# Transposes of both halves of a piece in one visit, with new planner rules and a reordered opening

## The chip, the cores and the metric

The kernel runs on one core of one Trainium2 chip. The metric is the device time of one execution in microseconds (us), the median of several runs. TensorE (PE in the profile, PEld for its weight loads) multiplies matrices and writes PSUM, VectorE (DVE), ScalarE (ACT) and GpSimd (POOL) work element by element, and SyncE (SP) issues most DMAs.

## The reference

One block of a hybrid sequence model over 1040 tokens (16 learned ones and 1024 frames) of width 1024: a mixer with four mLSTM heads and four retention heads, and a gated MLP with a causal convolution of three taps. Cut to what matters here:

```python
h = concat([meta, x])                                   # (1, 1040, 1024)
h = h + token_mixer(rmsnorm(h, norm_mix_g), ...)
h = h + channel_mixer(rmsnorm(h, norm_ffn_g), ...)
return rmsnorm(h, norm_final_g)[:, 16:]

def token_mixer(u, ...):
    proj = u @ w_in              # per head: q, k (128 wide), v (256), o or g (256), mLSTM gates
    ...
    h_ml = sigmoid(ml_o) * head_norm(mlstm_chunkwise(q, k, v, li, lf), ml_norm_g)
    h_rt = silu(rt_g) * head_norm(retention_chunkwise(rq, rk, rv, log_gamma), rt_norm_g)
    return concat([h_ml, h_rt]) @ w_out

def channel_mixer(u, ...):
    return (silu(causal_dwconv(u @ w_up, ffn_conv_w)) * (u @ w_gate)) @ w_down
```

The recurrences carry a 128 x 256 state per head from chunk to chunk; `head_norm` takes mean and variance over the 256 values of a head.

## The kernel before, in words

**Products.** Tokens lie along the free dimension, features along the 128 partitions. Each float32 operand is split into a high part (`hi`, a ScalarE copy to float32r) and a low part (`lo`, a VectorE subtraction), and each product is made of three float32r matmuls, hi x hi, lo x hi and hi x lo (`mm3`, `mm3s`, L889 to L903). The large products go through a scheme of seven block products in place of eight (`wino_fm`, `v_steps`, later `Seven` and `seven`), with the weights' sums made on VectorE (`quartered`, L553). The scan of the heads, the transposes and the norms' sums use plain float32 matmuls.

**The opening (L1735 to L1810).** Five column ranges (`RNG`, L251: 144 and 128 columns first) are normalised one after the other. `norm_sums(r)` (L848) squares the inputs on ScalarE and VectorE, adds the squares, sums over partitions by matmuls (`pca`, L824), and takes a square root and a reciprocal (L826, L827). `norm_split(r)` (L872) spreads the result over the partitions by matmuls (`pra`, L836), scales the columns (L879) and splits them (L880, L884). `v0_split` (L905) splits head 4's value weights; the low parts `w0lo` are subtracted on GpSimd. `v4_group(c)` (L919) makes the values of chunk c from them: high columns times high weights, high times low, then low times high; in group 1 the call `between`, which is `norm_sums(1)`, stands ahead of the last third. `need(("q4", 0), 1)` calls for the query weights' parts (`parts`, L472; the subtractions are the `lo_q` of L479). `last[...]` keeps an instruction, and `after(x, last[...])` orders x behind it on its engine without a semaphore. In this part the framework's own scheduler fixes the order on each engine, by readiness and place in the program.

**The planner (L1815 to L1917).** From head 4's output gate on, the kernel's own planner deals out the work. A model (`watch`, L132) follows the engines' loads with a price per instruction; on TensorE each change between float32 and float32r matmuls is charged (L178). Between products (`slot`, L1701) tasks from the list `side` are started, first come first served, if the task's own condition holds. A rule from `RULES` is in force for each stage (output gate `o`, query and key `q`, value `v`, `vp`, by head or pair). Its seven numbers are: how many weight parts ahead count as near, how long ahead of its data a waiting task may be resumed, the backlog of VectorE and ScalarE from which other pending tasks wait, the backlog from which no new task is started, the most tasks per slot, the order of the queues, and the most tasks with matmuls per slot. `done` holds what the model thinks finished, and when. `drain(nm, keep)` forces all but the last `keep` tasks.

**The scan.** For head h and each of nine chunks, `scan_a` (L1508) makes scores and `scan_b` (L1551) the state update `u` (bank "upd") and the output `n` (bank "num"). PSUM has eight banks: two each for `pa` and `pb` (products), one each for `sA`, `num`, `upd` and `tr`. After the chunks of one of three pieces (`PIECES`: 400, 384 and 256 tokens), `post_steps` (L1591) takes the head norm's statistics (`stats`) and then, per half b of the 256 features, `half(b)` (L1623): the chunks' outputs are transposed on TensorE into the bank `tr`, VectorE multiplies them with the norm's weight and the gate (`mix_into`, L1637) into a buffer `mx` (three of them), and ScalarE's queue stores it to DRAM (`mxd`, L1655). Head 7's mixes go straight to the operands of the next product (`wact`). Each half starts when bank `tr` is free by the model and its half of the gate (`sig`) is ready.

Of the kernel before, what the change touches and what calls it, by code (L numbers as in the profile page):

```python
# [47 lines left out]

RULE = (3, 0.5, 3.0, 2.5, 2, 0, 1)
RULES = {  # L50
# [19 lines left out]
}  # L70

# [18 lines left out]
def body(ctx, tc, h_in, vecs, cst, mask_in, rot, w_v0, w_vp, w_g, w_out, w_up, w_gate, w_down, out):  # L90
# [41 lines left out]
    def watch(ins):  # L132
# [25 lines left out]
        if dma:  # L158
            load[eng] = t + (0.4 if eng == "SP" else 0.1)
            size = n * o.ap[0][1] * 4e-6  # L160
            if eng == "SP":
                load["wire"] = max(load["wire"], t + 1.8) + size / 0.3 * (2 if "scr" in str(rd) else 1)
                end = load["wire"]
            else:
                load["wire"] += size / 0.3
                end = t + 1.8 + size / 0.15
        else:
            if eng == "PE":
                if F32 not in [x.dtype for x in ins.ins]:
                    c = max(0.107, 0.004 + 0.000445 * n)  # L170
                elif o.ap[0][1] == 32:
                    c = 0.13
                elif getattr(ins, "is_transpose", False):
                    c = 0.109
                else:
                    c = 2 * max(0.11, 0.00084 * n)
                whole = F32 in [x.dtype for x in ins.ins]
                c += 0.1 * (whole != kindof[0])  # L178
                kindof[0] = whole
                end = t + c + 0.165  # L180
            elif eng == "DVE":
                c = 0.07 + 0.00105 * n + (0.06 if "ScalarPtr" in kind else 0.0)
                end = t + c + 0.085
            elif eng == "Activation":
                c = 0.045 + 0.00093 * n + 0.1 * (len(ins.ins) - 1)
                f = ins.func.name if hasattr(ins, "func") else "Copy"
                if f in TABLES and f != table[0]:
                    table[0] = f
                    c += 1.3
                end = t + c + 0.1  # L190
            else:
                c = 0.15 + 0.0017 * n
                end = t + c
            load[eng] = t + c
            fin[0] = max(fin[0], end)
# [276 lines left out]
    def parts(key, pairs, src):  # L472
        for i, (hi, lo) in enumerate(pairs):
            m = AC.copy(hi, src[:, i * HB:(i + 1) * HB])
            if not dealt[0]:
                after(m, last["first"])
        yield
        for i, (hi, lo) in enumerate(pairs):
            V.tensor_tensor(lo, src[:, i * HB:(i + 1) * HB], hi.bitcast(F32), ALU.subtract)  # L479
        done.add(key)  # L480

    def pairs_of(nm, n):
# [365 lines left out]
    def norm_sums(r):  # L848
        half, j0, j1 = RNG[r]
        n = j1 - j0  # L850
        xs = [xf[f"{half + 1}{i + 1}"][:, :, j0:j1] for i in (0, 1)]
        sq = [x[:, :, j0:j1] for x in sqs]
        m = AC.activation(sq[0], xs[0], AF.Square)
        if r:
            after(m, last["sqrt"])
        if r < 2:
            m = V.tensor_tensor(sq[1], xs[1], xs[1], ALU.mult)
            if r:
                after(m, last["scale"])
        else:  # L860
            after(AC.activation(sq[1], xs[1], AF.Square), last["sqrt"])
        if r == 1:
            ss = [x[:, k] for x in sq for k in range(4)]
        else:
            m = V.tensor_tensor(sq[0], sq[0], sq[1], ALU.add)
            if r:
                after(m, last["recip"])
            V.tensor_tensor(sq[0][:, 0:2], sq[0][:, 0:2], sq[0][:, 2:4], ALU.add)
            ss = [sq[0][:, k] for k in range(2)]
        norms[r] = xs, rms_sums(ss[0], 0, n, f"a{r}", tmp.tile([P, 5], F32, tag="rcol", name=f"rcola{r}"), "tr", ss[1:])  # L870

    def norm_split(r):  # L872
# [4 lines left out]
        for i, x in enumerate(xs):  # L877
            for k in range(4):
                last["scale"] = V.scalar_tensor_tensor(x[:, k], x[:, k], vec[:, V_MIX + 4 * i + k:V_MIX + 4 * i + k + 1], pr, ALU.mult, ALU.mult)  # L879
            m = AC.copy(parts_[i][0], x)  # L880
            if r == 0:
                last["first"] = m
        for x, (h_, l_) in zip(xs, parts_):
            last["pace"] = V.tensor_tensor(l_, x, h_.bitcast(F32), ALU.subtract)  # L884
        if r == 0:
            for i, x in enumerate(xs):
                V.tensor_copy(ug[:, 4 * i:4 * i + 4], x[:, :, :32])
# [17 lines left out]
    def v0_split():  # L905
        for i in range(2):
            after(AC.copy(w0hi[i], w0raw[i]), last["sqrt"])
            G.tensor_tensor(w0lo[i], w0raw[i], w0hi[i].bitcast(F32), ALU.subtract)

    def quads(dst, pv, n):  # L910
        yield
# [639 lines left out]
    def scan_b(h, c):  # L1551
# [12 lines left out]
        num, mv, den = outs[p]  # L1564
        num.append(v_chunk(h, c, nv))
        if c < NCH - 1:
            up = pp(f"u{h}_{c}", "upd")
            PE.matmul(up[:, :nv], kw[:L], v, start=True, stop=True)  # L1568
        pn = pp(f"n{h}_{c}", "num")
# [4 lines left out]
        if c < NCH - 1:  # L1574
# [3 lines left out]
            else:  # L1578
                r = c * H + h
                d = dec[:, r:r + 1] if h < H else float(np.exp(lg[h - H] * P))  # L1580
                V.scalar_tensor_tensor(C[:, :nv], state["C"][:, :nv], d, up[:, :nv], ALU.mult, ALU.add)
            state["C"] = C
        AC.copy(num[slot][:L], pn[:L, :nv])
        if h < H:
            G.tensor_copy(den[:L, c:c + 1], num[slot][:L, DV:VW])
# [5 lines left out]
    def post_steps(h, p):  # L1591
# [28 lines left out]
            m["num"] = num  # L1620
            done.add(("z", h, p))

        def half(b):  # L1623
            num = m["num"]
            done.discard("tr")
            tr = ps.tile([P, 512], F32, tag="tr", name=f"tr{h}_{p}_{b}")
            for i, c in enumerate(chs):
                c0, L = CH[c]
                PE.transpose(tr[:, c0 - t0:c0 - t0 + L], num[i][:L, b * P:(b + 1) * P], ident[:L, :L])  # L1629
            yield  # L1630
            a0 = max(t0, KEEP)
            w = t1 - a0
            g = (V_MLG if h < H else V_RTG) + (h % H) * 2 + b
            i = 2 * h + b

            def mix_into(dst, x0, x1):
                return V.scalar_tensor_tensor(dst, tr[:, x0 - t0:x1 - t0], vec[:, g:g + 1], sig(b, p)[:, x0 - a0:x1 - a0], ALU.mult, ALU.mult)  # L1637
            if h == 7:
                for q, o in (("A2", MA), ("B2", MB)):
                    x0, x1 = max(a0, o), min(t1, o + HB)  # L1640
                    if x0 < x1:
                        mix_into(wact(q, 6 + b)[:, x0 - o:x1 - o], x0, x1)
                if t1 > MB + HB:
                    scanned["mix", b] = mix_into(mm[:, i], MB + HB, t1)
                done.add("tr")
                return
            mx = mxp.tile([P, WMAX], F32, tag="mx", name=f"mx{h}_{p}_{b}", bufs=3)
            mix_into(mx[:, :w], a0, t1)
            done.add("tr")
            e = min(t1, MB + HB)  # L1650
            if e < t1:
                V.tensor_copy(mm[:, i], mx[:, e - a0:w])
                posted.add(i)
            yield from settle()
            AC.dma_start(mxd[i][:, a0 - MA:e - MA], mx[:, :e - a0])  # L1655
            stored.add((i, p))
        return [(stats, 0, lambda: ("n", h, chs[-1]) in done)] + [(lambda b=b: half(b), 1, lambda b=b: done.can(("z", h, p), "tr") and ("sig", h, b) in done and "meta" not in done) for b in range(2)]

    side = []

    def tasks(h):
# [4 lines left out]

        def rb(c):
            v = [("v", h, int(c > 4))] if h not in (4, 7) else []
            return lambda: (h, c) in pre and done.can(("pre", h, c), *(turn if c == 0 else [("n", h, c - 1)] + v))
        A = [(lambda c=c: scan_a(h, c), 1, ra(c)) for c in range(NCH)]  # L1670
        B = [(lambda c=c: scan_b(h, c), 1, rb(c)) for c in range(NCH)]
        posts = [post_steps(h, p) for p in range(3)]
# [76 lines left out]
    norm_sums(0)  # L1749
    v0_split()  # L1750
    norm_split(0)
    v4_group(1, next(ring0), lambda: norm_sums(1))
    need(("q4", 0), 1)
    norm_split(1)
    v4_group(0, next(ring0))
    v4_group(2, next(ring0))
    norm_sums(2)
# [65 lines left out]
        return [(f, 0, lambda: "gates" in done)]  # L1823
    reset()
    load.update({"DVE": 7.0, "Activation": 5.5})
    done["tr"] = 0.0
    pinned[0] = True
    before.clear()
    go(o_steps(4))
    for p, (a, b) in enumerate(PAIRS):  # L1830
# [25 lines left out]
        go(steps[10:12])  # L1856
        side += cv[1:2]
        go(steps[12:])
        drain(f"sig{a}", 4)
        scan, halves_ = tasks(b)  # L1860
        if b < H:
            side += cv[2:3] + scan[:3] + cv[3:] + scan[3:10]
# [668 lines left out]
```

## Time and profile before

| | us |
|---|---|
| median of 3 runs | 1527.99 (1526.26 to 1529.33) |
| the profiled execution | 1527.2 |
| its span, first to last instruction | 1525.4 |
| TensorE busy | 1489.9 (98%) |
| VectorE busy | 1090.1 (71%) |
| ScalarE busy | 755.6 (50%) |

The profiled execution took 1.8 us more than its span, and 0.8 less than the median. The granted TensorE clock is 0.994 over the span. The rows of the views say which engine an instruction ran on, its line in the kernel, what it writes and reads, its start and its length; what stands in brackets at a row's end is how long its engine had been idle, and what ended that. Starts of matmuls are exact; their lengths overlap, since they are pipelined, so a matmul's price is read from start to start. A transpose on TensorE is a matmul, too.

### The profile page before, as it was taken

What the parts mean: (1) busy time and instruction counts of PE and PEld (TensorE: products, weight loads), DVE (VectorE), ACT (ScalarE), POOL (GpSimd) and SP (SyncE); (2) the same over time, 40 slices, a digit from 0 to 9 for tenths busy, and PEclk for the clock granted to TensorE, in tenths of its full rate; (3) what the DMA queues carried; (4) which work ended last, traced back from release to release, by engine and by line L of the source; (5) the groups of instructions that cost most, each with busy time, mean ns of one, the idle gap of its engine ahead of it and who ended that gap; (6) DMA issues with size and microseconds to landing.
All of it is one profiled execution on the core that took longest, in us unless ns stands there. A gap on an engine that the chain in (4) does not pass through costs nothing.

```text
span 1525.4 us, 25488 instructions
## 1 busy us (share of the span) xinstructions
PE 1489.9 (98%) x9929; PEld 1350.0 (88%) x9929; DVE 1090.1 (71%) x2087; ACT 755.6 (50%) x1453; POOL 73.6 (5%) x153
## 2 busy tenths in 40 slices
PE   6999999999999999999999999999999999999997
PEld 6998999999999999986888988999999999888887
DVE  7785868678777677856867787767666666778657
ACT  4465655554655455553454565444444444444443
POOL 1000000000000000000000001222220000000000
PEclk9999999999999999999999999999999999999999
DMA  6022255323532355696333247888772224933313
GB/s 232 8 88 51 86 159 194 111 82 114 186 119 98 125 166 189 195 398 255 111 112 134 80 124 241 197 208 200 189 183 77 83 79 160 369 105 110 97 42 111
DMA packets 104586, 223.81 MB, mean 147 GB/s; under 512 B 10520, under 2 KB 33760, under 8 KB 104288
## 3 DMA queue, kind: packets, MB, share of 16 engines
q1 hardware_dynamic: 89824, 191.68, 37.7%
q0 software_dynamic: 8448, 23.07, 7.6%
q10 hardware_dynamic: 6192, 7.41, 1.4%
q8 instruction: 78, 1.28, 0.4%
q14 instruction: 44, 0.36, 0.1%
HBM read 178.05 MB, written 67.15 MB: 161 GB/s over the span
## 4 chain that ended last, share of the span: by engine, by line
PE 89%; DVE 6%; DMA 2%; ACT 2%; issue 1%; SPq 0%; DVEq 0%; ACTq 0%
PE pdx L902 3%; PE pdx L901 3%; PE pdx L900 3%; PE pup_x L901 2%; PE pup_x L902 2%; PE pga_x L900 2%; PE pup_x L900 2%; PE pga_x L901 2%; PE pga_x L902 2%; PE pdy L902 2%; PE pdy L901 2%; PE pdy L900 2%; PE n L1570 2%; PE pwx L902 2%; PE u L1568 2%; PE pv L940 2%
## 5 line engine op out<-in xcount | busy, mean ns | idle before, releaser
L780 ACT CAST hi_up<-raw_up 128x512 fp32r<-128x512 f32 (+1 forms) x52 | 36.4, 719 | 107.4 <-PE pga_z L901 61.1
L781 DVE TENSOR_TENSOR lo_ga<-fraw_ga,hi_ga 128x512 fp32r<-128x512 f32 (+1 forms) x52 | 41.9, 809 | 37.3 <-ACT hi_ga L780 37.1
L781 DVE TENSOR_TENSOR lo_up<-raw_up,hi_up 128x512 fp32r<-128x512 f32 (+1 forms) x52 | 41.3, 810 | 38.0 <-ACT hi_up L780 37.2
L900 PE MATMUL pup_x<-uh_g,hi_up 128*128 128x256 f32 (+1 forms) x240 | 67.2, 282 | 1.2 <-ACT uh_g L1928 1.2
L901 PE MATMUL pup_x<-ul_g,hi_up 128*128 128x256 f32 (+1 forms) x240 | 67.4, 282 | 0.1
L902 PE MATMUL pup_x<-uh_g,lo_up 128*128 128x256 f32 (+1 forms) x240 | 66.4, 282 | 0.0
L781 DVE TENSOR_TENSOR lo_d<-rd,hi_d 128x1024 fp32r<-128x1024 f32 (+1 forms) x34 | 37.7, 1114 | 32.8 <-ACT hi_d L780 32.7
L780 ACT CAST hi_ga<-fraw_ga 128x512 fp32r<-128x512 f32 (+1 forms) x52 | 36.4, 719 | 45.3 <-PE pup_z L901 21.9
L902 PE MATMUL pdx<-uh_d,lo_d 128*128 128x512 f32 (+1 forms) x156 | 57.9, 375 | 0.0
L901 PE MATMUL pdx<-ul_d,hi_d 128*128 128x512 f32 (+1 forms) x156 | 57.8, 374 | 0.0
L780 ACT CAST hi_d<-rd 128x1024 fp32r<-128x1024 f32 (+1 forms) x34 | 32.3, 959 | 49.3 <-PE pdy L901 32.5
L902 PE MATMUL pdy<-uh_d,lo_d 128*128 128x512 f32 x132 | 51.9, 393 | 0.0
L901 PE MATMUL pdy<-ul_d,hi_d 128*128 128x512 f32 x132 | 51.7, 392 | 0.0
L900 PE MATMUL pdx<-uh_d,hi_d 128*128 128x512 f32 (+1 forms) x156 | 48.5, 372 | 0.0
L900 PE MATMUL pdy<-uh_d,hi_d 128*128 128x512 f32 x132 | 47.9, 389 | 0.0
L900 PE MATMUL pga_x<-uh_g,hi_ga 128*128 128x512 f32 x120 | 47.5, 396 | 0.0
L901 PE MATMUL pga_x<-ul_g,hi_ga 128*128 128x512 f32 x120 | 47.5, 396 | 0.0
L900 PEld LDWEIGHTS pup_x<-uh_g,hi_up 128*128 128x128 f32 x240 | 45.3, 189 | 2.3 <-ACT uh_g L1928 1.4
L902 PE MATMUL pga_x<-uh_g,lo_ga 128*128 128x512 f32 x120 | 47.1, 393 | 0.0
L901 PEld LDWEIGHTS pup_x<-ul_g,hi_up 128*128 128x128 f32 x240 | 45.4, 189 | 1.0 <-DVE ul_g L1929 0.3
L902 PEld LDWEIGHTS pup_x<-uh_g,lo_up 128*128 128x128 f32 x240 | 44.8, 189 | 0.8
L1637 DVE SCALAR_TENSOR_TENSOR mx<-tr,vec,sig 128x386 f32<-128x386 f32 (+2 forms) x42 | 24.0, 572 | 20.7 <-PE tr L1629 16.0
(1684 smaller groups left out, 5752.4 us busy)
## 6 DMA issues: line engine op xcount, KB each, us to landing
raw_up<-w_up_d SPq DMA_DIRECT2D x22, 512.0 KB, 4.4
fraw_ga<-w_gate_d SPq DMA_DIRECT2D x22, 512.0 KB, 4.1
acts<-cv SPq DMA_DIRECT2D x44, 256.0 KB, 4.2
wsd<-w_down_d POOLq DMA_DIRECT2D x44, 256.0 KB, 6.6
rd<-wsd SPq DMA_DIRECT2D x22, 512.0 KB, 3.6
raw_w<-w_out_d SPq DMA_DIRECT2D x20, 512.0 KB, 6.8
wsw<-raw_w SPq DMA_DIRECT2D x32, 256.0 KB, 3.7
raw_m<-w_out_d SPq DMA_DIRECT2D x14, 512.0 KB, 4.0
```

Source lines behind the costliest of these rows:

```text
L780: AC.copy(hi[:, o:o + n], x)
L781: V.tensor_tensor(lo[:, o:o + n], x, hi[:, o:o + n].bitcast(F32), ALU.subtract)
L900: m.append(PE.matmul(pt, ah, xh_, start=first and k == 0, stop=False, skip_group_check=True))
L901: PE.matmul(pt, ah, xl_, start=False, stop=False, skip_group_check=True)
L902: m.append(PE.matmul(pt, al, xh_, start=False, stop=last and k == n - 1, skip_group_check=True))
L940: PE.matmul(pv[:, :nv], u[:, kb % 4, j0:j0 + L], (w0hi, w0lo)[j][kb // 4][:, o:o + nv], start=i + j + kb == 0, stop=i == 1 and kb == KB - ...
L1568: PE.matmul(up[:, :nv], kw[:L], v, start=True, stop=True)
L1570: PE.matmul(pn[:L, :nv], pt[:L, :L], v, start=True, stop=c == 0)
L1637: return V.scalar_tensor_tensor(dst, tr[:, x0 - t0:x1 - t0], vec[:, g:g + 1], sig(b, p)[:, x0 - a0:x1 - a0], ALU.mult, ALU.mult)
```

## The change

It has four parts. `post_steps` gets `both()` in place of `half(b)`: it transposes both halves in one visit, the first into bank `tr`, the second into bank `upd`, mixes them one after the other and then issues both stores. It starts when both banks are free and both halves of the gate are ready. For this `scan_b` marks `upd` as taken and free, and is held back while it is taken, unless it makes no update. Seventeen of nineteen planner rules have other numbers, and the model charges 0.13 in place of 0.1 for a change of kind. One `drain` keeps three tasks in place of four where the list is shorter. In the opening, `w0lo` is subtracted on VectorE behind the second norm's squares (`v0_lows`); the first columns' low parts come behind it, the query weights' low parts and the third norm's square sums come behind the last scaling before them in the program, and `norm_sums(1)` is called inside `norm_split(0)`; `norm_split(1)` stands ahead of the call for the query weights.

```diff
-    ("o", 0): (4, 0.3, 3.0, 2.5, 2, 0, 3),
-    ("o", 1): (3, 0.0, 2.0, 1.5, 2, 1, 3),
-    ("o", 2): (4, 0.5, 3.0, 4.0, 1, 1, 2),
-    ("o", 3): (2, 0.8, 3.0, 2.5, 1, 1, 1),
-    ("o", 4): (4, 0.3, 4.5, 1.5, 1, 0, 1),
...
+    ("o", 0): (4, 0.3, 3.0, 2.5, 4, 0, 2),
+    ("o", 1): (3, 0.8, 2.0, 1.5, 3, 0, 2),
+    ("o", 2): (3, 0.5, 3.0, 1.5, 2, 1, 2),
+    ("o", 3): (3, 0.8, 3.0, 1.5, 2, 1, 1),
+    ("o", 4): (4, 0.3, 4.5, 1.5, 2, 0, 2),
...
-                c += 0.1 * (whole != kindof[0])
+                c += 0.13 * (whole != kindof[0])
...
         for i, (hi, lo) in enumerate(pairs):
-            V.tensor_tensor(lo, src[:, i * HB:(i + 1) * HB], hi.bitcast(F32), ALU.subtract)
+            m = V.tensor_tensor(lo, src[:, i * HB:(i + 1) * HB], hi.bitcast(F32), ALU.subtract)
+            if not dealt[0]:
+                after(m, last["scale"])
...
             m = V.tensor_tensor(sq[0], sq[0], sq[1], ALU.add)
             if r:
-                after(m, last["recip"])
+                after(m, last["scale"])
...
+        if r == 0:
+            norm_sums(1)
+            v0_lows()
         for x, (h_, l_) in zip(xs, parts_):
             last["pace"] = V.tensor_tensor(l_, x, h_.bitcast(F32), ALU.subtract)
+            if r == 0:
+                after(last["pace"], last["w0lo"])
...
             after(AC.copy(w0hi[i], w0raw[i]), last["sqrt"])
-            G.tensor_tensor(w0lo[i], w0raw[i], w0hi[i].bitcast(F32), ALU.subtract)
+
+    def v0_lows():
+        for i in range(2):
+            last["w0lo"] = V.tensor_tensor(w0lo[i], w0raw[i], w0hi[i].bitcast(F32), ALU.subtract)
+            after(last["w0lo"], last["square"])
...
         if c < NCH - 1:
+            done.discard("upd")
             up = pp(f"u{h}_{c}", "upd")
...
             state["C"] = C
+            done.add("upd")
...
-        def half(b):
+        def both():
             num = m["num"]
             done.discard("tr")
-            tr = ps.tile([P, 512], F32, tag="tr", name=f"tr{h}_{p}_{b}")
-            for i, c in enumerate(chs):
-                c0, L = CH[c]
-                PE.transpose(tr[:, c0 - t0:c0 - t0 + L], num[i][:L, b * P:(b + 1) * P], ident[:L, :L])
+            done.discard("upd")
+            tr = [ps.tile([P, 512], F32, tag=x, name=f"{x}{h}_{p}") for x in ("tr", "upd")]
+            for b in range(2):
+                for i, c in enumerate(chs):
+                    c0, L = CH[c]
+                    PE.transpose(tr[b][:, c0 - t0:c0 - t0 + L], num[i][:L, b * P:(b + 1) * P], ident[:L, :L])
             yield
...
             yield from settle()
-            AC.dma_start(mxd[i][:, a0 - MA:e - MA], mx[:, :e - a0])
-            stored.add((i, p))
+            for i, mx in out:
+                AC.dma_start(mxd[i][:, a0 - MA:e - MA], mx[:, :e - a0])
+                stored.add((i, p))
...
-            return lambda: (h, c) in pre and done.can(("pre", h, c), *(turn if c == 0 else [("n", h, c - 1)] + v))
+            return lambda: (h, c) in pre and done.can(("pre", h, c), *(turn if c == 0 else [("n", h, c - 1)] + v), *(["upd"] if c < NCH - 1 else []))
...
-    v4_group(1, next(ring0), lambda: norm_sums(1))
+    v4_group(1, next(ring0))
+    norm_split(1)
     need(("q4", 0), 1)
-    norm_split(1)
...
-        drain(f"sig{a}", 4)
+        drain(f"sig{a}", 4 if b < H else 3)
```

More of the change, by code (lines that the diff above doesn't have):

```diff
@@ L857, in norm_sums @@
             m = V.tensor_tensor(sq[1], xs[1], xs[1], ALU.mult)
+            last["square"] = m
             if r:
@@ L1632, in half @@
             w = t1 - a0
[L1633 to L1646, printed above, removed]
@@ L1647, in half, with mix_into @@
-            mx = mxp.tile([P, WMAX], F32, tag="mx", name=f"mx{h}_{p}_{b}", bufs=3)
-            mix_into(mx[:, :w], a0, t1)
-            done.add("tr")
-            e = min(t1, MB + HB)
-            if e < t1:
-                V.tensor_copy(mm[:, i], mx[:, e - a0:w])
-                posted.add(i)
+            e = min(t1, MB + HB)
+            out = []
+            for b in range(2):
+                g = (V_MLG if h < H else V_RTG) + (h % H) * 2 + b
+                i = 2 * h + b
+                def mix_into(dst, x0, x1):
+                    return V.scalar_tensor_tensor(dst, tr[b][:, x0 - t0:x1 - t0], vec[:, g:g + 1], sig(b, p)[:, x0 - a0:x1 - a0], ALU.mult, ALU.mult)
+                if h == 7:
+                    for q, o in (("A2", MA), ("B2", MB)):
+                        x0, x1 = max(a0, o), min(t1, o + HB)
+                        if x0 < x1:
+                            mix_into(wact(q, 6 + b)[:, x0 - o:x1 - o], x0, x1)
+                    if t1 > MB + HB:
+                        scanned["mix", b] = mix_into(mm[:, i], MB + HB, t1)
+                    done.add(("tr", "upd")[b])
+                    continue
+                mx = mxp.tile([P, WMAX], F32, tag="mx", name=f"mx{h}_{p}_{b}", bufs=3)
+                mix_into(mx[:, :w], a0, t1)
+                done.add(("tr", "upd")[b])
+                if e < t1:
+                    V.tensor_copy(mm[:, i], mx[:, e - a0:w])
+                    posted.add(i)
+                out.append((i, mx))
@@ L1654, in half @@
             yield from settle()
-            AC.dma_start(mxd[i][:, a0 - MA:e - MA], mx[:, :e - a0])
-            stored.add((i, p))
-        return [(stats, 0, lambda: ("n", h, chs[-1]) in done)] + [(lambda b=b: half(b), 1, lambda b=b: done.can(("z", h, p), "tr") and ("sig", h, b) in done and "meta" not in done) for b in range(2)]
+            for i, mx in out:
+                AC.dma_start(mxd[i][:, a0 - MA:e - MA], mx[:, :e - a0])
+                stored.add((i, p))
+        return [(stats, 0, lambda: ("n", h, chs[-1]) in done), (both, 1, lambda: done.can(("z", h, p), "tr", "upd") and {("sig", h, 0), ("sig", h, 1)} <= done.keys() and "meta" not in done)]
@@ L1825, in body @@
     load.update({"DVE": 7.0, "Activation": 5.5})
-    done["tr"] = 0.0
+    done["tr"] = done["upd"] = 0.0
     pinned[0] = True
```

24 rows, old and new, of the table RULES are left out of this document.

## The prediction, as it was put on record

> **What bounds the kernel now.** I read the page first, then the granted clock and busy time by stretch, then the timeline of the first 40 us, then TensorE's waits, then the transposes. The page says which engine carries the time.
>
> ```profile
> span 1525.4 us, 25488 instructions
> PE 1489.9 (98%) x9929; PEld 1350.0 (88%) x9929; DVE 1090.1 (71%) x2087; ACT 755.6 (50%) x1453; POOL 73.6 (5%) x153
> ...
> PE 89%; DVE 6%; DMA 2%; ACT 2%; issue 1%; SPq 0%; DVEq 0%; ACTq 0%
> ```
>
> TensorE is busy 98% of the span and holds 89% of the chain that ended last. A change that leaves its matmuls alone can win only where it waits or runs below full clock. The table by stretch shows where that is.
>
> ```profile
> core 0: us, PE busy (x) PEld busy (x) DVE busy (x) ACT busy (x) POOL busy (x), PEclk, DMA share, GB/s
> ...
> 13.00:28.00 15.00, 11.87 (x66) 9.10 (x66) 12.81 (x26) 8.49 (x15) 1.93 (x1) 1.00 0.91 326
> 28.00:40.00 12.00, 12.00 (x87) 12.00 (x87) 11.17 (x21) 4.64 (x8) 0.09 (x1) 0.86 0.01 2
> ...
> 150.00:690.00 540.00, 536.22 (x4188) 505.00 (x4188) 391.86 (x876) 296.44 (x622) 8.81 (x55) 1.00 0.48 160
> 690.00:720.00 30.00, 26.53 (x108) 20.01 (x107) 19.59 (x36) 11.19 (x17) 0.00 (x0) 0.89 0.75 275
> ```
>
> There are three places. Before 28 us the first norms keep TensorE waiting. From 150 to 690 us only 3.8 of 540 us are idle. At the mixer's end, 690 to 720 us, 3.5 us are idle and the clock of 0.89 costs 30 x 0.11 = 3.3 us more.
>
> **The first norms.** The timeline of the first 40 us, with one later row for a price:
>
> ```profile
> 4.74 0.76 DVE L857 TENSOR_TENSOR sqr<-x 128x576 f32<-128x576 f32 x1 [3.87 <-DMA x<-h_in_d]
> ...
> 10.11 2.43 POOL L908 TENSOR_TENSOR w0lo<-w0raw,w0hiq 128x1056 fp32r<-128x1056 f32 x1 [8.96 <-ACT w0hiq L907]
> ...
> 12.49 2.44 POOL L908 TENSOR_TENSOR w0lo<-w0raw,w0hik 128x1056 fp32r<-128x1056 f32 x1
> 12.79 2.68 DVE L857 TENSOR_TENSOR sqr<-x 128x512 f32<-128x512 f32 x1
> ...
> 16.34 0.75 DVE L884 TENSOR_TENSOR u12l<-x,u12h 128x576 fp32r<-128x576 f32 x1
> 17.01 2.49 DVE L479 TENSOR_TENSOR lo_q<-raw_q,hi_q 128x512 fp32r<-128x512 f32 x4
> ...
> 19.42 0.15 DVE L827 RECIPROCAL rcola<-rcola 128x1 f32<-128x1 f32 x1
> 19.69 1.23 DVE L865 TENSOR_TENSOR sqr<-sqr,sqr 128x1024 f32<-128x1024 f32 x1
> ...
> 22.98 0.49 PE L836 MATMUL pra<-cs,rcola 128*128 128x128 f32 x2
> 23.50 2.15 DVE L879 SCALAR_TENSOR_TENSOR x<-x,vec,pra 128x128 f32<-128x128 f32 x8 [0.41 <-PE pra L836]
> 26.24 0.71 PE L836 MATMUL pra<-cs,rcola 128*128 128x128 f32 x4 [1.22 <-DVE rcola L827]
> 27.88 1.08 PE L940 MATMUL pv<-w0hiq,u11h 128*128 128x264 f32 x4 [0.93 <-ACT u11h L880]
> 28.68 1.66 DVE L879 SCALAR_TENSOR_TENSOR x<-x,vec,pra 128x256 f32<-128x256 f32 x4
> ...
> 67.15 1.26 DVE L1787 TENSOR_TENSOR uS2l<-x,uS2h 128x1056 fp32r<-128x1056 f32 x1
> ```
>
> What leaves: two subtractions on GpSimd. While they run, VectorE's square takes 2.68 us for 512 columns and ends 0.54 us after GpSimd; the same line took 0.76 for 576 without it, so 0.68 for 512. That gives back 2.0 us of a chain TensorE waits on. What comes: the two subtractions on VectorE, 2 x 1.26 = 2.52 us by the row at 67.15. They stand ahead of the query's low parts (u11l, u12l, two of 0.75). The four lo_q subtractions, 2.49 us, which now stand ahead of the second reciprocal, move behind the second scaling, and so does the square sum of the third norm (1.23 us at 19.69 and a smaller one).
>
> So VectorE is through with the square, the two subtractions and the low parts at about 12.79 + 0.68 + 2.52 + 1.50 = 17.5, where it now is at 17.1. The reciprocal can start there at the latest, instead of at 19.42: 1.9 us earlier. In the trace the broadcast matmul (22.98) stands 3.4 us behind the reciprocal, because TensorE's queue holds the first value group ahead of it. That group gets its last operand at 17.5 instead of 17.1, so the queue may hold the broadcast back to the same 23. If it doesn't, the second scaling starts about 18.5 (a broadcast of 0.49 and the steps around it). The bounds for that scaling are therefore 18.5 and 23.5, five microseconds better or nothing.
>
> Against this stands what is put behind it. From the second scaling's end (25.65) to the third's start (28.68) VectorE now needs 3.0 us. In the changed order lo_q and the sum, 2.49 + 1.23 and half of that again, fall into that interval, and the low parts of the second columns too (two of 0.67, from 0.75 for 576). So the third scaling may come up to 1.8 us later than now, or 2 us earlier if lo_q is taken last. TensorE has the second value group and two query groups, 24 matmuls each, some 9 us at the 0.12 from start to start that the rows of the next part show, to bridge it. VectorE is busy 12.81 of 15 us here, so it can't give all of the five.
>
> The clock belongs to this term: 0.86 from 28 to 40 is 12 x 0.14 = 1.7 us lost, right after the waits of 1.22 and 0.93. If the second columns come three microseconds earlier, the waits shrink and part of this is kept. The Trainium skill, "TensorE: Matmul & The Clock Gate", section "Part 1: The HAM clock gate", says the clock halves after a wholly idle window of about 3.4 us; by that, two gaps of 2.15 us together would lose nothing and nothing could be won here. The trace has the loss after the shorter gaps, so the row decides. I take -2.5 us for the start, from bounds of -6.7 (five, and the clock) and +1.8.
>
> **One visit instead of two.** 48 visits of transposes become 24. What does a visit cost besides its transposes? Two from TensorE's timeline, one with two transposes and one with four of which the first has 16 rows:
>
> ```profile
> 148.96 0.28 PE L902 MATMUL pv0y<-hi_vp,u12l 128*128 128x256 f32 x1
> 149.17 0.23 PE L1629 MATMUL tr<-cs,vz 16*128 16x16 f32 x1
> 149.33 0.55 PE L1629 MATMUL tr<-cs,v4lo 128*128 128x128 f32 x3
> 149.63 0.36 PE L900 MATMUL pv0y<-hi_vp,u12h 128*128 128x256 f32 x1
> 149.84 0.27 PE L901 MATMUL pv0y<-lo_vp,u12h 128*128 128x256 f32 x1
> ```
>
> ```profile
> 157.87 0.28 PE L901 MATMUL pv0x<-lo_vp,uS2h 128*128 128x256 f32 x1
> 157.99 0.28 PE L902 MATMUL pv0x<-hi_vp,uS2l 128*128 128x256 f32 x1
> 158.11 0.38 PE L1629 MATMUL tr<-cs,v4hi 128*128 128x128 f32 x2
> 158.25 0.37 PE L900 MATMUL pv0x<-hi_vp,uS2h 128*128 128x256 f32 x1
> 158.45 0.28 PE L901 MATMUL pv0x<-lo_vp,uS2h 128*128 128x256 f32 x1
> ```
>
> Product matmuls start 0.12 apart. From 157.99 to 158.45 are 0.46 us; less two such steps, 0.22 is left for two transposes, 0.11 each. The other: 0.88 less 0.24 is 0.64, of which three take 0.33 and the 16-row one 0.31. So a plain visit has next to no price of its own (0.01), and only the 16-row pieces may have 0.2 at the entry, once per head and half. The planner charges 0.10 for each change of kind, soon 0.13: it believes in 24 x 2 x 0.13 = 6.2 us that TensorE doesn't have to give. Bounds: 24 x 0.01 = 0.2 and 8 x 0.2 + 0.2 = 1.8. I take -0.3.
>
> TensorE's waits from 87 to 720 us:
>
> ```profile
> PE s L1523 <- DVE pt L1547: 2.6, 1, 2.6
> PE pwy L901 <- DVE wr L1288: 1.8, 1, 1.8
> PE u L1568 <- DVE C L1581: 1.5, 2, 0.9
> PE tr L1629 <- DVE mx L1637: 1.5, 3, 1.1
> PE pwy L900 <- ACT wr L1288: 1.3, 1, 1.3
> ```
>
> The fourth row is the wait of a second half for the one bank "tr". With a bank for each half it goes: -1.5 us. In its place the second half holds "upd", which the scan's state update needs; the planner now holds that update back instead of letting TensorE run into it, so what is late is a scan step, not TensorE.
>
> The stores of the mixed pieces become the next thing late:
>
> ```profile
> L1637 DVE SCALAR_TENSOR_TENSOR mx<-tr,vec,sig x42: 476/613/622, 149.9 to 632.8; 128x386 f32<-128x386 f32 x14, 128x384 f32<-128x384 f32 x14, 128x256 f32<-128x256 f32 x14
> ...
>   DMA mxd<-mx: 1.9, 2
> ...
> DMA to landing us min/median/max: 2.0/3.1/6.0
> ```
>
> There are three buffers "mx". Now a buffer is reused three visits later; then a visit takes two, and the second piece's second half reuses the first's, whose store is issued only after both halves are mixed. Queued behind a blocked mix on VectorE are the evacuations of the product banks, and TensorE waits for those. The first half's transposes last 0.7 (149.17 to 149.88 above); with two mixes of 0.61 the store goes out at about 2.0 and lands at 5.1 by the median. A next visit, which waits for both banks and so comes some 2.3 later, has its second mix ready at 2.3 + 2.0 = 4.3. That is 0.8 us blocked, twice a head, for the seven heads that store: 11 us of VectorE, which has room (391.86 of 540). A bank's 12 matmuls last 12 x 0.118 = 1.4 us, so blocks shorter than this hide behind the other bank. I count +1.0, from 0 to the rival's 11.
>
> **The mixer's end.** Head 7 has six visits, each half waiting for the bank; three rounds fewer let the last mixes leave VectorE about 2 us earlier, when it is less crowded. Of the 1.8 + 1.3 us of waits for wr and 3.3 of clock I count -1.0, between 0 and -5.
>
> **The new rules** change how many tasks go beside each product and when. Between 120 and 690 us the waits that they could remove are those of the first and third row above, 2.6 + 1.5 = 4.1. They can as well add as much. I count 0, plus or minus 4; the planner's dearer change of kind, which the rows above do not bear out, is no help.
>
> **The sum.** -2.5 - 0.3 - 1.5 + 1.0 - 1.0 = -4.3. The profiled execution took 1527.2, 1.8 beside its span, and is 0.8 below the median of the three runs, 1527.99. So 1522.9 for such an execution and 1523.7 for the median.
>
> **The rivals.** (a) *The stores block VectorE.* For it: landings up to 6.0 us, and two buffers per visit. At 6.0 the block is 3.7 us, 2.3 more than a bank hides; if that meets a third of the 14 reuses, 4.7 x 2.3 = 11 us, in place of the +1.0: 1533.7. It decides from a landing of about 3.7 us on. Against it: the median landing is 3.1, and just two waits on this buffer show now.
> (b) *The start does not change.* The opening is ordered by readiness, and the change gives only orders; if lo_q and the sums take the place of what they made way for, the start's term is 0 and the time 1526.2, within what can be told apart.
> (c) *More is won.* The start gives five (2.5 more) and the mixer's end keeps its clock (3.5 more): 1517.7. For it: both losses follow short waits.
>
> **How the numbers follow.** Forecast 0.42, rival (a) 0.26, (b) 0.10, (c) 0.22. About 0.2% (3.1 us) is what a measurement of this kernel can tell from no change. The forecast's own range, by the rules' plus or minus 4, is 1519.7 to 1527.7. It gives 0.34 faster and 0.08 same; (c) is faster; (b) gives 0.02, 0.07 and 0.01; (a) slower. In all 0.58 faster, 0.15 same, 0.27 slower. The range goes from (c) less the rules' 4 (1514) to (a) at 1533.
>
> **What would show it.** Right: the square at L857 near 0.7 us, the two w0lo subtractions on VectorE near 1.26, the second scaling at 19 to 22 us, and TensorE's first steady stretch starting well before 27.88; 24 visits with transposes at 0.11 each; no wait of tr for mx. Wrong: the third scaling later than 28.68 with a new wait of TensorE near 31 to 35; waits of mix instructions for mxd stores of several microseconds, with product matmuls waiting behind them; new waits of u for upd.

## The result and the profile after

| | before | after |
|---|---|---|
| median of 4 runs, us | 1528.09 (1526.26 to 1529.33) | 1545.14 (1543.31 to 1547.58) |
| ratio of the times | | 1.0113 [1.0101, 1.0125] |
| the profiled execution, us | 1527.2 | 1547.6 |
| its span, us | 1525.4 | 1545.5 |

The kernel became 17 us slower; 4.3 us faster was forecast, and the range ended at 1533. From the page of the changed kernel, the chain that ended last:

```profile
PE 85%; DVE 8%; DMA 4%; ACT 2%; issue 1%; POOL 0%; SPq 0%; DVEq 0%; ACTq 0%
```

VectorE holds 8% of the chain that ended last instead of 6%, DMA 4% instead of 2%, TensorE 85% instead of 89%. Where this happens is seen at three places of TensorE's work: the last matmul of head 4's output gate (`po4x`, from the timeline), the first of the output product (`pwx`) and the first of the MLP (`pup`, both from the groups by form, where "675.2 to 705.7" are the first and last start). Before:

```profile
98.32 0.28 PE L902 MATMUL po4x<-u22h,lo_o 128*128 128x256 f32 x1
```

```profile
L900 PE MATMUL pwx<-wone,hi_w x32: 388/396/586, 675.2 to 705.7; 128*128 128x512 f32 x32
...
L900 PE MATMUL pup<-xh,hi_up x32: 277/282/366, 848.3 to 863.3; 128*128 128x256 f32 x16, 128*128 128x258 f32 x16
```

And after:

```profile
117.49 0.28 PE L910 MATMUL po4x<-u22h,lo_o 128*128 128x256 f32 x1
```

```profile
L908 PE MATMUL pwx<-wone,hi_w x32: 388/394/585, 705.4 to 733.5; 128*128 128x512 f32 x32
...
L908 PE MATMUL pup<-xh,hi_up x32: 277/282/366, 869.0 to 884.0; 128*128 128x256 f32 x16, 128*128 128x258 f32 x16
```

At the end of the first gate the new kernel is 19.2 us behind, at the output product 30.2, at the MLP 20.7, and at the end 20.1 (these two executions lie further apart than the medians). So 19 us are lost up to the end of the first gate, the scan loses 11 more, and the end of the mixer gives 9.5 back. From 13 us to the end of that gate (98.6 us before, 117.8 after) TensorE is idle 15.8 us instead of 3.7, and busy 89.0 us instead of 81.9 with nearly the same matmuls (645 and 641 records), at a mean clock of 0.92 instead of 0.98. So 12.1 us of the 19.2 are idle time, and 7.1 are matmuls that take longer. By stretch, before:

```profile
core 0: us, PE busy (x) PEld busy (x) DVE busy (x) ACT busy (x) POOL busy (x), PEclk, DMA share, GB/s
40.00:55.00 15.00, 15.00 (x129) 15.00 (x129) 9.69 (x21) 5.91 (x10) 0.00 (x0) 1.00 0.01 2
55.00:87.00 32.00, 31.42 (x269) 30.48 (x268) 30.22 (x39) 18.86 (x31) 3.30 (x2) 1.00 0.22 68
87.00:125.00 38.00, 33.99 (x264) 31.93 (x263) 25.28 (x75) 18.87 (x40) 0.32 (x3) 0.98 0.32 84
```

and after, in the same columns, with three stretches whose rows of before stand in the prediction:

```profile
13.00:28.00 15.00, 12.72 (x71) 10.03 (x71) 10.08 (x23) 6.87 (x12) 0.00 (x0) 1.00 0.79 269
28.00:40.00 12.00, 9.88 (x66) 9.66 (x66) 5.53 (x13) 4.44 (x8) 0.09 (x1) 0.86 0.20 72
40.00:55.00 15.00, 13.12 (x108) 12.92 (x109) 8.02 (x16) 5.20 (x8) 0.00 (x0) 1.00 0.00 1
55.00:87.00 32.00, 27.89 (x227) 27.29 (x226) 26.91 (x40) 13.24 (x22) 1.56 (x1) 0.97 0.01 1
87.00:125.00 38.00, 31.58 (x226) 29.54 (x225) 30.40 (x69) 19.82 (x34) 6.31 (x2) 0.84 0.24 84
...
690.00:720.00 30.00, 30.00 (x194) 25.97 (x193) 13.19 (x36) 16.68 (x33) 0.00 (x0) 1.00 1.05 398
```

The first stretch is better, as forecast: TensorE is busy 12.72 us instead of 11.87. From 28 us on each stretch loses: 2.1 us idle of 12, 1.9 of 15, 4.1 of 32, 6.4 of 38 (before 0, 0, 0.6 and 4.0), and in the last one the clock of 0.84 costs about 31.58 x 0.16 = 5.1 us of the busy time besides. VectorE is *less* busy than before where TensorE starts to wait (5.53 of 12 us, 8.02 of 15). It isn't overloaded there; it stands behind something. What that is shows in its timeline, with the rows of TensorE that it waits for or that wait for it. After:

```profile
12.87 0.68 DVE L859 TENSOR_TENSOR sqr<-x 128x512 f32<-128x512 f32 x1
13.47 1.25 DVE L919 TENSOR_TENSOR w0lo<-w0raw,w0hiq 128x1056 fp32r<-128x1056 f32 x1
...
17.42 0.15 DVE L829 RECIPROCAL rcola<-rcola 128x1 f32<-128x1 f32 x1
...
22.46 1.12 DVE L882 SCALAR_TENSOR_TENSOR x<-x,vec,pra 128x128 f32<-128x128 f32 x4 [4.89 <-PE pra L838]
...
24.61 2.49 DVE L479 TENSOR_TENSOR lo_q<-raw_q,hi_q 128x512 fp32r<-128x512 f32 x4
...
27.48 1.20 DVE L868 TENSOR_TENSOR sqr<-sqr,sqr 128x1024 f32<-128x1024 f32 x1
...
30.27 0.67 DVE L871 TENSOR_TENSOR sqr<-sqr 128x512 f32<-128x512 f32 x1
...
34.45 0.95 PE L826 MATMUL pca<-cs,sqr 128*128 128x1 f32 x8
...
35.73 0.17 DVE L829 RECIPROCAL rcola<-rcola 128x2 f32<-128x2 f32 x1 [0.63 <-ACT rcola L828]
...
38.35 0.61 PE L838 MATMUL pra<-cs,rcola 128*128 128x128 f32 x4
...
39.00 3.22 DVE L882 SCALAR_TENSOR_TENSOR x<-x,vec,pra 128x256 f32<-128x256 f32 x8 [3.10 <-PE pra L838]
...
53.81 3.36 DVE L882 SCALAR_TENSOR_TENSOR x<-x,vec,pra 128x272 f32<-128x272 f32 x8 [0.99 <-PE pra L838]
...
66.89 3.22 DVE L882 SCALAR_TENSOR_TENSOR x<-x,vec,pra 128x256 f32<-128x256 f32 x8 [1.42 <-PE pra L838]
70.03 1.29 DVE L479 TENSOR_TENSOR lo_o<-raw_o4a,hi_o 128x512 fp32r<-128x512 f32 x2
```

The same instructions before:

```profile
33.73 1.27 DVE L479 TENSOR_TENSOR lo_o<-raw_o4a,hi_o 128x512 fp32r<-128x512 f32 x2
...
42.68 1.23 DVE L865 TENSOR_TENSOR sqr<-sqr,sqr 128x1024 f32<-128x1024 f32 x1 [1.72 <-ACT sqr L861]
...
46.62 3.36 DVE L879 SCALAR_TENSOR_TENSOR x<-x,vec,pra 128x272 f32<-128x272 f32 x8
...
53.42 3.22 DVE L879 SCALAR_TENSOR_TENSOR x<-x,vec,pra 128x256 f32<-128x256 f32 x8 [0.99 <-PE pra L836]
```

One norm from start to end reads: the sum is done at 30.9, its matmul `pca` starts at 34.45, the reciprocal at 35.73, its broadcast `pra` at 38.35, the scaling at 39.00. The two passages through TensorE's queue, behind query products that stand ahead of them there, take 3.5 and 2.4 us. Before, the sums of the next norm started ahead of the scaling before it (the fifth's at 42.68, the fourth scaling at 46.62), so these passages ran beside other work: the fourth and fifth scaling stand 6.8 us apart. Now a sum may only start when the scaling before it has been issued, and the fourth and fifth stand 13.1 us apart. The third comes 10.3 us later than the 28.68 of before, the fourth 7.2, the fifth 13.5; and the output gate's low parts, which another line of the change (in `parts`) puts behind the last scaling, at 70.0 instead of 33.7. TensorE's longest waits from 13 to 125 us are those of the gate's products and of the value groups (`sig` is an evacuation of the gate, `rawk` of the key product, `u11h` and `u11l` are the high and low part of scaled columns; the columns are us in total, times, the longest):

```profile
PE po4x L908 <- ACT sig L982: 4.4, 1, 4.4
PE pv L952 <- ACT u11h L883: 3.9, 2, 2.6
PE po4x L908 <- ACT rawk L962: 3.1, 1, 3.1
PE pv L952 <- DVE u11l L890: 2.2, 1, 2.2
```

The 2.6 us end at 41.78 and are for the third norm's columns, scaled from 39.00 on. The 2.2 us end at 29.34 and are for the second norm's low part, which VectorE makes behind `lo_q` and the sum.

### The profile page after: what moved, and what is told of

Its sections match the earlier page's. It is cut to its first block, busy times and chain, and to the rows that moved or that the text cites. A ratio compares the mean times of both kernels' runs of the same rounds, so it can differ in the third digit from the quotient of the medians.

```text
span 1545.5 us, 25465 instructions
## 1 busy us (share of the span) xinstructions
PE 1495.7 (97%) x9929; PEld 1355.6 (88%) x9929; DVE 1089.3 (70%) x2089; ACT 756.3 (49%) x1454; POOL 73.3 (5%) x151
## 4 chain that ended last, share of the span: by engine, by line
PE 85%; DVE 8%; DMA 4%; ACT 2%; issue 1%; POOL 0%; SPq 0%; DVEq 0%; ACTq 0%
PE pdx L910 3%; PE pdx L909 3%; PE pdx L908 3%; PE pup_x L909 2%; PE pup_x L910 2%; PE pga_x L908 2%; PE pup_x L908 2%; PE pga_x L909 2%; PE pga_x L910 2%; PE pdy L910 2%; PE pdy L909 2%; PE pdy L908 2%; PE pwx L910 2%; PE n L1583 2%; PE pwx L908 2%; PE pwx L909 2%
## 5 line engine op out<-in xcount | busy, mean ns | idle before, releaser
L662 POOL DMA_DIRECT2D wsd<-w_down_d x33 | 19.9, 749 | 373.3 <-DVE s2up L2176 373.3
```

The source lines that it names most:

```text
L662: dep(G.dma_start(x, y), last["pace"], True)
```

## The experiments

Each ratio is to the kernel before, run on the same chip beside it, with its 95% interval. "The opening" is all that the change does ahead of the planner.

**The changed kernel with the old opening.** All edits of the opening undone; visits, rules and price of the change stay.

> The changed kernel with the whole opening of the kernel before: low value weights on GpSimd, query low parts free, square sums behind the reciprocal, the second norm's sums inside the first value group. Both-halves visits and new rules stay. In the two traces head 4's output gate ends 19.2 us later than before (117.5 against 98.3), the scan adds about 10 and the mixer's end gives about 9.5 back. Theory A, the opening carries the loss: about 1545 - 19 = 1526 us. Theory B, the loss is the planner's (visits and rules), and the opening's delay would be hidden later: 1540 or more.

Measured: 1530.01 us, 1.0027 [1.0018, 1.0037]. Of the 1.13% of the loss 0.86% goes with the opening, about 13 us.

**The opening alone**, put into the kernel before, with nothing else.

> The kernel before with the new opening alone, halves in visits of their own and old rules. Theory A: 1528 + 19 = 1547 us, as slow as the whole change or slower. Theory B: 1528 to 1533.

Measured: 1543.20 us, 1.0113 [1.0098, 1.0128]: the whole loss, 17 us. The parts don't add up (1.13 + 0.27% against 1.13%); why 4 us of the one are swallowed when the other is there was not followed.

**Square sums free again**, in the changed kernel:

```diff
             if r:
-                after(m, last["scale"])
+                after(m, last["recip"])
```

> The changed kernel, with the square sums of the third and later norms behind the reciprocal of the norm before, as they were, and not behind its scaling. Theory A1, these sums make each norm wait for the one before (third scaling at 39.0 where it was at 28.7): most of the 19 us comes back, 1528 to 1532 us. Theory A2, the low parts of the weights behind the scalings fill VectorE late (it gets the output gate's low parts only from 70 us on): less than 5 us come back, 1540 or more.

Measured: 1529.26 us, 1.0020 [1.0011, 1.0029]. One word takes back 14 us, as much as undoing the whole opening. Its timeline says more than its time:

```profile
34.96 3.23 DVE L882 SCALAR_TENSOR_TENSOR x<-x,vec,pra 128x256 f32<-128x256 f32 x8
...
47.34 3.36 DVE L882 SCALAR_TENSOR_TENSOR x<-x,vec,pra 128x272 f32<-128x272 f32 x8
...
54.34 3.22 DVE L882 SCALAR_TENSOR_TENSOR x<-x,vec,pra 128x256 f32<-128x256 f32 x8 [1.18 <-PE pra L838]
```

```profile
28.00:40.00 12.00, 12.00 (x83) 12.00 (x83) 10.11 (x21) 4.45 (x8) 0.09 (x1) 0.82 0.25 85
```

The third scaling is still 6.3 us late here, and TensorE is busy 12.00 of the 12 us around it: its query products cover that. The fourth and fifth are back within 1 us of the kernel before. So a third norm 6.3 us late costs TensorE no wait here; one 10.3 us late, in the changed kernel, costs the 2.6 us that end at 41.78. The line holds for the third, fourth and fifth norm; how the rest of the loss divides among them was not tried.

**Only the square sums late**, the reverse of this, in the kernel before:

```diff
-                after(m, last["recip"])
+                after(m, last["scale"])
```

> The kernel before with one word changed: the square sums of the third and later norms stand behind the scaling of the norm before them, not behind its reciprocal. Theory A1, this order by itself serialises the norms (sum, matmul, root, reciprocal, broadcast, scaling, one norm after the other): 1538 to 1545 us, the third scaling 8 to 11 us later than 28.7. Theory A3, it costs that only together with the query's low parts behind the scaling and the low value weights on VectorE: under 1532.

Measured: 1540.09 us, 1.0080 [1.0065, 1.0094], 12 us from this word alone. Its timeline has the same chain:

```profile
30.47 1.27 DVE L479 TENSOR_TENSOR lo_o<-raw_o4a,hi_o 128x512 fp32r<-128x512 f32 x2
...
36.88 3.22 DVE L879 SCALAR_TENSOR_TENSOR x<-x,vec,pra 128x256 f32<-128x256 f32 x8 [2.94 <-PE pra L836]
...
51.68 3.36 DVE L879 SCALAR_TENSOR_TENSOR x<-x,vec,pra 128x272 f32<-128x272 f32 x8 [1.02 <-PE pra L836]
...
64.94 3.22 DVE L879 SCALAR_TENSOR_TENSOR x<-x,vec,pra 128x256 f32<-128x256 f32 x8 [1.42 <-PE pra L836]
```

Scalings 14.8 and 13.3 us apart, although the output gate's low parts are early (30.47). This word is shown to be both needed for most of the loss and enough for most of it.

**Low parts of the weights free again**, in the changed kernel: the two lines with `after(m, last["scale"])` in `parts` taken out.

> The changed kernel, with the low parts of query and output gate weights free to go when ready, and not behind a scaling. Theory A1 (the sums): less than 5 us come back, 1540 or more. Theory A2 (the low parts): 1528 to 1535 us.

Measured: 1539.39 us, 1.0087 [1.0072, 1.0102]: 4 us come back while the sums are still late. With free sums (1.0020) and with the whole old opening (1.0027) the times agree, so low parts behind a scaling cost nothing that can be told where the sums are free.

**Only the low parts of the value weights moved**: the kernel before with `v0_lows` on VectorE, `norm_sums(1)` inside `norm_split(0)` and `norm_split(1)` ahead of `need`; sums and query parts as they were.

> The kernel before with that part of the new opening which is left when the two costly orders are taken out: low value weights on VectorE behind the second squares, first low parts behind them, the second norm's split ahead of the call for the query weights; sums behind the reciprocal, query low parts free. The prediction took 2.5 us for the opening, from a square that no longer waits for GpSimd (2.68 to 0.68 us in the changed trace). Theory F, that is a gain by itself: 1522 to 1525 us. Theory G, the broadcast waits in TensorE's queue behind the first value group (22.0 in the changed trace where it was 23.0) and the later norms see nothing of it: 1525.5 to 1528.

Measured: 1525.92 us, 0.9995 [0.9986, 1.0004]. The interval holds 1: the idea behind the opening, without what was tied to it, gains less than can be told.

**Rules alone.** The kernel before with all new rules and the price of 0.13.

> The kernel before with the new rules and the new price of a change of kind alone; halves in visits of their own, old opening. Theory C: 1529 to 1533 us. Theory D: 1524 to 1527. If rules and visits only fit each other (theory E), both this and the run with the visits alone are above 1530.

Measured: 1529.97 us, 1.0025 [1.0016, 1.0034], nearly 4 us slower. The three places of the result's section tell rules and opening apart. With the rules alone they stand at 99.90, 686.4 and 850.6 us, so 1.6, 11.2 and 2.3 behind the kernel before; with the opening alone at 113.55, 692.5 and 864.3, so 15.2, 17.3 and 16.0 behind. Nearly all that the scan loses and the end of the mixer gives back is thus the rules' doing, and the opening's loss is there by the end of the first gate.

**Visits alone.** The kernel before with `both()`, the holding back of state updates and the shorter `drain`, old rules and price; only `("v", 7)` has the new numbers, since with the old ones head 7's first operand would be read before it is stored.

> The opening, the rules and the price of a change of kind as before; of the planner's part only the visits of both halves, and the one new rule for head 7's value product (with the old one head 7's first operand isn't stored when it is read). With the old opening the whole planner's part cost 3.6 us (1530.0 against 1526.4). Theory C, the new rules cost that and the visits are about free: 1523 to 1527 us. Theory D, the visits cost it (two banks held at once, stores of mixed pieces later): 1529 to 1533.

Measured: 1575.09 us, 1.0320 [1.0306, 1.0334], 48 us slower, outside both expected ranges. Visits with the new rules cost 0.27%, the new rules alone 0.25%: with rules made for them the visits cost next to nothing, with others much. TensorE's waits from 87 to 740 us begin:

```profile
PE pvm L720 <- DMA raw_vm<-w_vp_d: 17.5, 4, 12.1
```

The row is a weight load that came late: one wait of 12.1 us, and 17.5 of the 48 us in all. These loads take as long from issue to landing as before (a median of 4.9 us, 5.1 before), but the last is issued at 546.0 instead of 516.9. Why the order of tasks pushes the load back, and where the rest goes, was not followed.

**Rules of head 7 alone**, in the kernel before:

```diff
-    ("o", 7): (2, 0.5, 3.0, 2.5, 1, 0, 1),
+    ("o", 7): (4, 0.5, 3.0, 4.0, 2, 0, 1),
-    ("v", 7): (3, 0.8, 3.0, 4.0, 2, 1, 1),
+    ("v", 7): (4, 0.8, 3.0, 1.5, 2, 1, 3),
```

> The kernel before with two new rules only, those of head 7's value product and output gate. In the trace with the old opening head 7's scan runs ahead in the output gate's stage (its end 11.4 us later than before), and the output product then ends 9.0 us sooner against that: net 3.8 us won from the value product's end on, with the waits for wr at 708 to 712 us and the half clock behind them gone. Theory H, these two rules make that gain: 1521 to 1524 us. Theory I, the shorter list of visits does: 1526 to 1529.

Measured: **1522.45 us, 0.9972 [0.9962, 0.9982]**, the one version that beats both kernels. Its groups by form and its last stretch of the mixer:

```profile
L900 PE MATMUL pwx<-wone,hi_w x32: 388/394/585, 678.5 to 707.3; 128*128 128x512 f32 x32
...
L900 PE MATMUL pup<-xh,hi_up x32: 277/282/366, 842.7 to 857.7; 128*128 128x256 f32 x16, 128*128 128x258 f32 x16
```

```profile
690.00:720.00 30.00, 29.77 (x137) 23.71 (x136) 21.87 (x39) 13.86 (x21) 0.00 (x0) 1.00 0.76 284
```

The output product starts 3.3 us later than before, but runs almost without a gap (0.2 us idle of 30) and at full clock, and the MLP starts 5.6 us earlier. That is the pattern of the changed kernel (a later output product, and time given back behind it), without any new visit.

**Combinations.** Three kernels asked what more could be had: head 7's rules with the moved value parts; head 7's rules with the new rules of `("o", 0)`, `("q", 1)`, `("q", 2)`; and the changed kernel with the old opening and the old rules of `("o", 4)`, `("q", 0)`, `("vp", 0)`, `("o", 1)`.

> The two rules of head 7 (1522.5 us, 4.3 won) with the harmless part of the new opening (1525.9, 0.9 won, within the interval). If the two add up: 1521 to 1522 us. If the opening's part is nothing: 1522.5 again.

> The two rules of head 7 and three more of the new rules, for the stages in which the kernel with the new rules alone caught up on the kernel before (head 0's output gate by 1.1 us, head 1's query by 1.2, head 2's query by 2.0). If a rule's effect belongs to its stage: 1518 to 1521 us. If the effect hangs on what the rules ahead left over: 1523 or more.

> Visits of both halves and new rules with the old opening (1530.0 us), but the old rules in four stages in which that kernel fell behind: head 4's output gate, head 0's query, the first value product, head 1's output gate. If the loss of the planner's part lies in these rules: 1523 to 1526 us. If it comes from the visits or hangs on the whole set: 1529 or more.

Measured: 1525.38 us, 0.9992 [0.9984, 1.0001]; 1529.72, 1.0020 [1.0011, 1.0028]; 1527.70, 1.0002 [0.9992, 1.0013]. The first and the third lie outside both of their expected ranges. None beats head 7's rules alone, and the gain of those two rules is lost beside a change of the opening that by itself does nothing measurable. A rule's effect is not a property of its stage that can be added up; which step of the planner turns it was not settled.

## Why the prediction was wrong

**The opening, -2.5 within -6.7 and +1.8: this step failed**, and it carries the miss (+17 alone). What the step said of the part it looked at is right. The square took 0.68 us (2.68 before), the two `w0lo` on VectorE 1.25 each (1.26 taken), the reciprocal started at 17.42 (17.5 "at the latest"), and the broadcast was held back by the first value group in TensorE's queue, as feared: the second scaling came at 22.46, after 4.89 us of waiting for `pra`, at the late end of "18.5 and 23.5". Rival (b)'s "start does not change" is what the moved subtractions by themselves measure in time (0.9995).

The error is in the paragraph on what is put behind that scaling. It counted `lo_q`, the sums and the low parts as VectorE's work between two scalings and found at most 1.8 us (its own rows, 2.49 + 1.23 + 0.62 + 1.34 = 5.7, are 2.7 above the 3.0). The wait that the change adds is a dependency, and its price is the whole way from the sum to the next scaling: sum, `pca`, root, reciprocal, `pra`, two of them in TensorE's queue. In the changed kernel that way is 27.48 to 39.00, 11.5 us, of which the two additions and the reciprocal are 2.0 (1.20, 0.67, 0.17). And the step, like the section on the change, speaks of the third norm only, where the order stands in a function for all norms (`norm_sums(r)`) and holds for the third, fourth and fifth. Its "9 us" of TensorE's work do cover a third scaling that is 6.3 us late (the square sums freed), but not one that is 10.3 us late, where TensorE waits 2.6 us; the fourth and fifth scaling and the output gate behind them, which the step left out, carry the larger waits. Its mark for being wrong, "the third scaling later than 28.68 with a new wait of TensorE", is met: the scaling comes at 39.00, and the new wait ends at 41.78, later than the "31 to 35" named. The largest waits, 4.4 and 3.1 us, are the output gate's and come in the stretches from 55 to 125 us.

**Visits, -0.3: nothing was saved.** A merged visit, from TensorE's timeline after:

```profile
181.04 0.28 PE L910 MATMUL pv0x<-hi_vp,uS2l 128*128 128x256 f32 x1
181.16 0.38 PE L1645 MATMUL tr<-cs,v4hi 128*128 128x128 f32 x2
181.38 0.38 PE L1645 MATMUL upd<-cs,v4hi 128*128 128x128 f32 x2
...
181.72 0.27 PE L909 MATMUL pv0y<-lo_vp,uS1h 128*128 128x256 f32 x1
```

0.68 us less two steps of 0.12 is 0.44 for four transposes: twice the 0.22 of the old visit. That a plain visit has next to no price of its own is right; the 0.2 for the pieces with 16 rows is not saved either: in the merged visit at 172.19 us the second half's 16-row transpose stands 0.46 us ahead of the next product (172.83 to 173.29), as in the old visit (149.17 to 149.63). **The wait of tr for mx, -1.5: wrong.** It is still there, and the stores land a little later (the prediction's rows have 2.0/3.1/6.0). After, TensorE waits once for 1.8 us where it waited 1.5 us in three times; landings are 2.1/3.4/7.2, and the view of the tile `mx` has, of VectorE's idle time before its instructions (us, times):

```profile
  DMA mxd<-mx: 5.1, 3
```

**Stores, +1.0:** VectorE waits 5.1 us for them, 3.2 more than before, in three places and not in 14; rival (a), 11 us, did not come about. What of the 3.2 reaches the kernel's time was not measured apart. **The mixer's end, -1.0 within 0 and -5: mis-sized, and for the wrong reason.** The waits for `wr` are gone, and the clock is 1.00 from 690 to 720 us and on to 750, past the output product's new start at 705.4; but two rules do that without any visit (0.9972, the MLP 5.6 us earlier), so "three rounds fewer" is not needed for it. **Rules, 0 plus or minus 4:** the bound held, +0.25% alone. All that is not opening came to +0.27%, where the terms from the visits on gave -1.8 us: that part alone, 1528.09 x 1.0027 = 1532.2, would just have been inside the range.

## What to carry to other kernels

An order between two instructions of one engine can cost all that lies between the second one and the next use of its result, through every queue on that way, and not only the busy time of the engine on which it stands; here a less busy VectorE was the sign of it. Ask of such a line how often it is executed: one word in a function called for every norm cost 12 us, and only the first of the three norms that it holds back had been looked at. The planner's rules did not add up here: two of seventeen gained 4 us, all of them lost 4, and adding others to the two lost the gain.

## What the runs showed of the hardware

The clock fell to half after quite short stops. In the kernel with only the sums late, TensorE's longest waits from 13 to 125 us (us in total, times, the longest) and two of its stretches are:

```profile
PE pv L940 <- ACT u11h L880: 4.1, 2, 2.8
PE po4y L900 <- ACT sig L970: 2.7, 1, 2.7
```

```profile
98.00:101.00 3.00, 0.95 (x8) 0.73 (x7) 2.27 (x4) 2.15 (x4) 0.00 (x0) 1.00 0.47 176
101.00:110.00 9.00, 6.32 (x30) 6.02 (x29) 6.95 (x19) 5.83 (x10) 0.00 (x0) 0.50 0.00 0
```

TensorE stands 2.05 of the first 3 us, and in the next 9, which hold the wait of 2.7, it runs at 0.50: on 6.32 us of busy time some 3.2 are lost, more than any wait. No wait in this part is longer than 2.8. The Trainium skill, "TensorE: Matmul & The Clock Gate", section "Part 1: The HAM clock gate", names at least one idle window of about 3.4 us for the half clock; by that none of these stops could have caused it, and the trace does not agree. Reckoned in the same way the clock takes 5.1 us from 87 to 125 in the changed kernel, and 33.99 x 0.02 = 0.7 before; these two stretches do not hold the same work.
